# A third raw-weight buffer around the first norm, and a free choice of engine for four low parts

## The chip, the cores and the metric

The kernel runs on one core of one Trainium2 chip. The metric is the device time of one execution in microseconds, as the median of several runs. Inputs, outputs and all arithmetic that counts are 32-bit floating point.

## The reference

A decoder trunk of two layers on 512 tokens of width 1024. Each layer projects x once, runs four groups of attention heads side by side (A forgetting attention, B multi-head latent attention, C stick-breaking attention, D sliding-window attention with grouped keys and values), normalises each group, and sums them through one output projection. A layer norm, a gated feed-forward network of width 2816 and a second layer norm follow.

```python
for l in range(DEPTH):                                  # 2
    h = x @ w_in[l]                                     # split into the inputs of A, B, C, D
    ...                                                 # out_a, out_b, out_c, out_d: (1, 512, 256) each
    y = _group_rmsnorm(concat(out_a, out_b, out_c, out_d), mix_g[l]) @ w_o[l]
    x = _layernorm(ALPHA * x + y, ln1_g[l], ln1_b[l])
    f = (silu(x @ w_gate[l]) * (x @ w_up[l])) @ w_down[l]
    x = _layernorm(ALPHA * x + f, ln2_g[l], ln2_b[l])
```

## The kernel before

**Products in three passes.** TensorE multiplies a 32-bit value as two parts: a high part, which is the value rounded to the faster matmul type (`fp32r`), and a low part, which is the rest. Each product is three passes: high by high, high by low, low by high. So every weight chunk that arrives in a raw buffer is *split*: an engine casts it to the high part (ScalarE mostly, line 722; GpSimd sometimes, line 724), and VectorE or GpSimd subtracts that from the raw value for the low part (line 442). Both parts go into buffers of their own; the raw buffer is free once the low part is done.

**Buffers.** A `Ring` is a set of SBUF buffers. `r_raw` (`w_raw`) has 2 buffers of 128 x 1024 for raw weights, `r_hi` and `r_lo` (`w_hi`, `w_lo`) have 3 each for the parts. `r_qk` has 9 larger ones for queries, keys and later the hidden features. `r_vd` (`vd`) is a single buffer, as large as a raw one: it holds the values of the sliding group D, in both parts; later the paired tiles of the feed-forward network and the second norm's bias vector use it.

**The planner.** The program is written out by a list scheduler that runs when the kernel is built. Each operation has an engine, an estimated cost, the estimated times of what it depends on, and a priority. The scheduler always emits the operation that can start first, engine by engine, and so fixes the order in every engine's queue. On the chip each queue runs in that order, and semaphores hold an operation until its data are there, whatever time was planned for it. The function `best` chooses between engines by the earliest planned end: the later of the time at which the engine has worked off what is queued for it and the time at which the data are there, plus a cost. A low part of 1024 elements costs 69 + 1.042 x 1024 = 1136 ns on VectorE, to which 800 is added in this comparison, and 147 + 2.11 x 1024 = 2308 ns on GpSimd. A split that is further ahead than the next chunk has a low priority (`LOW`): other operations go first.

**Loads and splits.** All weight chunks stand in one list in the order in which TensorE uses them. `loader` loads them in that order, up to five positions ahead of the chunk in use, each when `raw_room` gives a buffer. All loads are issued from SyncE's queue (SP). `splitter` splits them in the same order, up to three positions ahead, each when `room` gives buffers for the parts; the next split starts in the plan only after the low part of the one before has its place.

**The stretch around the first norm.** The dense work of a layer is a list of units in a fixed order, ending its attention part with `wd wc load1 wab`: the output projection of group D, of group C, the load of the norm's vectors, and the projection of groups A and B together. After these come `up(0, 1)`, which computes the first two tiles of 128 hidden features, and then the paired tiles. In `wab` the four chunks of `w_o` belong to A (one of them split into a buffer of `r_v`) and B; it runs over token tiles 0 and 1 (t0, t1) for A then B, and then over t2 and t3. Each result is added onto x by VectorE (line 1743). As soon as a token tile has its four parts, `layernorm` runs on it: sums of squares on ScalarE (line 803), small operations of one element a partition on VectorE, two operations of 128 x 512 to centre and scale (line 853), and two more for the gain and the bias (line 858). TensorE then transposes the tile (line 751, two transposed halves a token tile), and ScalarE and VectorE write the two parts of it to `xT`. `up(0, 1)` uses four chunks, `w_gate` 0, `w_up` 0, `w_gate` 1, `w_up` 1, in that order, for tokens 0 to 255 and then for tokens 256 to 511. Their parts go into buffers of `r_qk`; their splits wait in the plan until group B's normalised output exists (`gate`).

Of the kernel before, what the change touches and what calls it, by code (L numbers as in the profile page):

```python
# [21 lines left out]
F32 = mybir.dt.float32  # L22
# [7 lines left out]
P = 128  # L30
# [16 lines left out]
GA, GB, GC, GD = range(4)  # L47
# [18 lines left out]
E_PE, E_ACT, E_DVE, E_POOL, E_SP = range(5)  # L66
# [11 lines left out]
def join(*deps):  # L78

    if any(x is None for x in deps):  # L80
        return None
    return tuple(map(max, zip(*deps))) if len(deps) > 1 else deps[0]
# [270 lines left out]
def trunk(ctx: ExitStack, tc: tile.TileContext, d):  # L353
# [15 lines left out]
    r_raw = Ring(sb, "w_raw", 2, [P, 1024], F32)  # L369
    r_hi = Ring(sb, "w_hi", 3, [P, 1024], F32R)  # L370
    r_lo = Ring(sb, "w_lo", 3, [P, 1024], F32R)
    r_qk = Ring(sb, "qk", 9, [P, 2, S], F32R)
    r_v = Ring(sb, "v", 2, [P, NT, 4, 2, 64], F32R)
    r_vd = Ring(sb, "vd", 1, [P, NT, 2, 2, 64], F32R)
# [23 lines left out]
    x = const.tile([P, NT, D], F32, name="x_res")  # L398
# [10 lines left out]
    def dma(out, in_, us=0.0, dep=NOW):  # L409

        e = yield Op(E_SP, 450.0, dep)
        nc.sync.dma_start(out=out, in_=in_)
        sched.dma = max(sched.dma, e[E_SP] + 800.0) + us * 1e3
        return mark(E_SP, sched.dma + 1100.0)
# [69 lines left out]
    def rows(src, k0, kt):  # L484
        return src[k0 * P:(k0 + kt) * P].rearrange("(k p) c -> p k c", p=P)
# [6 lines left out]
    class Chunk:  # L492


        def __init__(self, kt, n, parts, custom=None, rings=None, both=None, low=E_POOL, n_split=None, gate=None):
            self.kt, self.n, self.parts, self.custom = kt, n, parts, custom
            self.r_hi, self.r_lo = rings or (r_hi, r_lo)
            self.both, self.n_split, self.low, self.gate = both, n_split or n, low, gate
            self.raw = self.part = self.dep = self.loaded = None

        weight = 1

        def raw_room(self):
            return r_raw.ready()

        def view(self, tile_, n):
            return tile_[:, :self.kt * n].rearrange("p (k n) -> p k n", n=n)

        def load(self):
            self.raw = r_raw.take()  # L510
            e = NOW
            for k0, k1, c0, c1, src in self.parts:
                size = (k1 - k0) * (c1 - c0) * (2 if c1 - c0 < P else 1)
                e = yield from dma(self.view(self.raw.tile, self.n)[:, k0:k1, c0:c1], src, 1.46 * size / 1024, self.raw.dep)
            self.loaded = e
# [171 lines left out]
    def use(chunk):  # L687

        queue["used"] = max(queue["used"], chunk.pos)
        return (yield lambda: chunk.dep)  # L690

    def done(chunk_list, dep):
        for c in chunk_list:
            c.give(dep)

    def dense_op(cost, dep):
        return Op(E_PE, cost, dep, 1)
# [168 lines left out]
    def layer(l):  # L866
# [5 lines left out]
        at = {}  # L872
# [635 lines left out]
        class Uses:  # L1508


            def __init__(self, held, n):
                self.held, self.joint = held, Joint(n, held.give)
# [209 lines left out]
            return out  # L1722


        added = {(t, c): Joint(3) for t in range(NT) for c in range(2)}

        def out_proj(*groups, last=None):

            cs = {g: [Chunk(1, D, [(0, 1, 0, D, rows(d["w_o"][l], 2 * g + k, 1))],
                            both=r_v if len(groups) > 1 and g == groups[0] and k == 0 else None) for k in range(2)]  # L1730
                  for g in groups}
            chunks.extend(c for pair in cs.values() for c in pair)
            blocks = ((0, 1), (2, 3)) if len(groups) > 1 else ((0, 1, 2, 3),)

            def add(g, t, c, ps, dep, st, done_):
                yield lambda: at.get(("rs", g))
                yield lambda: x_dep[t]
                if st is not None:
                    yield lambda: added[t, c].dep
                rs = ops[g][1]  # L1740
                csl = slice(c * 512, c * 512 + 512)
                e = yield Op(E_DVE, 663.0, join(dep, at["rs", g], x_dep[t]))
                DVE.scalar_tensor_tensor(  # L1743
                    out=x[:, t, csl], in0=ps.tile, scalar=rs[:, t:t + 1], in1=x[:, t, csl], op0=ALU.mult, op1=ALU.add,
                    accum_out=st[:, c:c + 1] if st is not None else None,
                )
                ps.give(e)
                if st is not None:
                    done_[c] = e
                    if c == 0:  # L1750
                        last(t, st, e, lambda: done_.get(1))
                else:
                    added[t, c].add(e)

            def unit():
                for half in blocks:
                    for g in groups:
                        final = last if g == groups[-1] else None
                        if half[0] == 0:
                            ready = NOW  # L1760
                            for c in cs[g]:
                                ready = join(ready, (yield from use(c)))
                            yield lambda: at.get(("mix", g))
                        mix = ops[g][0]
                        if final and half[0] == 0:
                            yield lambda: r_b.whole()
                            new_xT(r_b.close())
                        for t in half:
                            st, done_ = None, {}
                            if final:  # L1770
                                yield lambda: NOW if final.loaded else None
                                st = sm.tile([P, 13], F32, name="lnst")
                            for c in range(2):
                                csl = slice(c * 512, c * 512 + 512)
                                yield lambda: r_d.ready()
                                ps = r_d.take()
                                e = yield dense_op(6 * 216.0, join(at["mix", g], ready, ps.dep))
                                for k in range(2):
                                    for i, (a, b) in enumerate(PASSES):
                                        mm(ps.tile, mix.tile[:, k, b, t * P:(t + 1) * P], cs[g][k][a][:, 0, csl],  # L1780
                                           start=(k == 0 and i == 0), stop=(k == 1 and i == 2))
                                spawn(add(g, t, c, ps, e, st, done_), 1 if final is None else 0, 0)
                        if half[-1] == NT - 1:
                            mix.give(e)
                            done(cs[g], e)
            return unit
# [82 lines left out]
        def up(*js):  # L1869
            cs = {}  # L1870
            for j in js:
                for n in ("w_gate", "w_up"):
                    cs[n, j] = Chunk(KT, P, [(0, KT, 0, P, rows(d[n][l][:, j * P:(j + 1) * P], 0, KT))],
                                     rings=(r_qk, r_qk) if len(js) > 1 else None, low=E_DVE if len(js) > 1 else None,
                                     gate=(lambda: ("mix", GB) in at) if len(js) > 1 else None)
            chunks.extend(cs.values())
            toks = HALVES if len(js) > 1 else (ALL,)

            def unit():
                ps, ready = {}, {}  # L1880
                for tok in toks:
                    for j in js:
                        for n in ("w_gate", "w_up"):
                            if tok.start == 0:
                                ready[n, j] = yield from use(cs[n, j])
                                ring = r_d if len(js) > 1 else (r_s if n == "w_gate" else r_u)
                                yield lambda: ring.ready()
                                ps[n, j] = ring.take()
                            xr = yield lambda: x_ready(tok)
                            for k in range(KT):  # L1890
                                e = yield from fm_piece(ps[n, j].tile, cs[n, j], slice(0, P), xs, k, tok, KT, tok.start == 0,
                                                        join(xr, ready[n, j], ps[n, j].dep))
                            if tok.stop == S:
                                done([cs[n, j]], e)
                        if tok.stop < S:
                            continue
                        yield lambda: g_ready(j)
                        gs[j] = g_tile(j)
                        spawn(hidden(j, ps["w_gate", j], ps["w_up", j], e), 0, 0)
            return unit  # L1900
# [230 lines left out]
        low = E_DVE  # L2131
# [140 lines left out]
```

## Time and profile before

| what | value |
|---|---|
| median of 3 runs | 1220.42 us (1219.75 to 1221.94) |
| profiled execution | 1220.06 us, span 1218.3 us |
| mean granted TensorE clock | 0.992 |
| TensorE busy | 1180.2 us, 97% of the span |
| VectorE busy | 892.1 us, 73% |
| ScalarE busy | 685.7 us, 56% |
| GpSimd busy | 241.4 us, 20% |

The span runs from the first to the last instruction of the profiled execution; the time of the execution is a little longer. In the rows below, PE is TensorE's matmuls, PEld its weight loads, DVE VectorE, ACT ScalarE, POOL GpSimd, SP SyncE with the loads that it issues (`SPq`). A row of the timeline gives the start, the time taken, the engine, the line, the operation, what it writes `<-` what it reads, the shape, and in brackets how long the engine had been idle and for what. A row of the waits gives the total in us, how often, and the longest. A row by tile or line gives the count and the least, median and greatest time of one in ns. The first norm of layer 0 lies at about 235 to 270 us, that of layer 1 at about 840 to 875.

### The profile page before, as it was taken

Reading aid. Unit: us, or ns where it says so; the run is one execution under the profiler, and the core shown is the slowest. Engines: PE = TensorE matmul, PEld = TensorE weight load, DVE = VectorE, ACT = ScalarE, POOL = GpSimd, SP = SyncE. Lnnn points to the kernel's source line nnn. Section 1 sums busy time; section 2 is a strip of 40 time slices with the busy share of each in tenths; the row PEclk is TensorE's granted clock in tenths of the full one; section 3 lists DMA queues with packets and bytes.
Section 4 is the critical chain, followed back from the end, with each engine's and each line's share of the span. In section 5 each row is a group of like instructions: output and inputs, shape, how many; then the busy total and the mean of one; then the engine's idle time right before and its main releaser. Section 6 shows DMA issues by size and latency. Waiting matters only on the chain.

```text
span 1218.3 us, 20162 instructions
## 1 busy us (share of the span) xinstructions
PE 1180.2 (97%) x7589; PEld 1069.5 (88%) x7589; DVE 892.1 (73%) x1699; ACT 685.7 (56%) x1441; POOL 241.4 (20%) x243
## 2 busy tenths in 40 slices
PE   8999999989999999999999999999899999999996
PEld 7979878779999989998799797778899989899985
DVE  5669668799896649873655895788998947499626
ACT  4759869456564325553356797684665634256421
POOL 3552765300000000000034536543000000000001
PEclk9999999999999999999999999999999999999999
DMA  6312230423333133324233211203233341343341
GB/s 201 88 47 63 57 104 12 128 87 87 105 105 120 48 128 105 105 92 130 72 71 87 57 53 56 87 27 113 87 90 119 96 131 51 108 119 88 104 138 70
DMA packets 112162, 110.75 MB, mean 91 GB/s; under 512 B 9792, under 2 KB 94656, under 8 KB 112064
## 3 DMA queue, kind: packets, MB, share of 16 engines
q1 hardware_dynamic: 112064, 109.45, 29.9%
q8 instruction: 60, 0.98, 0.3%
q14 instruction: 38, 0.31, 0.1%
HBM read 107.34 MB, written 2.10 MB: 90 GB/s over the span
## 4 chain that ended last, share of the span: by engine, by line
PE 79%; DVE 9%; ACT 5%; issue 3%; POOL 2%; DMA 0%; POOLq 0%; SPq 0%; DVEq 0%; ACTq 0%
PE ps L464 76%; PE ps L1557 1%; DVE x_res L1743 1%; POOL w_lo L442 1%; PE ps L751 1%; DVE xT L442 1%; DVE qk L442 1%; ACT temp L1445 1%; DVE pt L442 1%; ACT pt L1363 1%; DVE x_res L858 1%; ACT xT L722 0%; DVE qk L444 0%; DVE temp L1306 0%; DVE augk L1092 0%
## 5 line engine op out<-in xcount | busy, mean ns | idle before, releaser
L464 PE MATMUL ps<-xT,w_hi 128*128 128x256 f32 (+1 forms) x1128 | 215.5, 318 | 0.0
L464 PEld LDWEIGHTS ps<-xT,w_hi 128*128 128x128 f32 x1128 | 162.4, 191 | 11.4
L464 PE MATMUL ps<-w_hi,qk 128*128 128x512 f32 (+1 forms) x560 | 171.5, 388 | 0.0
L464 PE MATMUL ps<-xT,w_lo 128*128 128x256 f32 (+1 forms) x888 | 166.0, 304 | 0.0
L722 ACT CAST w_hi<-w_raw 128x1024 fp32r<-128x1024 f32 (+2 forms) x91 | 92.8, 1021 | 108.1 <-PE ps L464 90.5
L442 POOL TENSOR_TENSOR w_lo<-w_raw,w_hi 128x1024 fp32r<-128x1024 f32 (+4 forms) x66 | 120.9, 1837 | 106.4 <-ACT w_hi L722 76.3
L442 DVE TENSOR_TENSOR w_lo<-w_raw,w_hi 128x1024 fp32r<-128x1024 f32 x47 | 57.6, 1225 | 111.6 <-ACT w_hi L722 111.5
L464 PEld LDWEIGHTS ps<-xT,w_lo 128*128 128x128 f32 x888 | 123.7, 191 | 7.3
L464 PEld LDWEIGHTS ps<-w_hi,qk 128*128 128x128 f32 x560 | 104.6, 189 | 20.9
L464 PE MATMUL ps<-w_hi,mix 128*128 128x512 f32 x352 | 110.1, 394 | 3.1 <-DVE xT L442 1.8
L464 PE MATMUL ps<-w_lo,qk 128*128 128x512 f32 (+1 forms) x280 | 108.2, 387 | 0.0
L1911 ACT COPY temp<-ps 128x256 f32<-128x256 f32 x120 | 44.7, 373 | 85.2 <-PE ps L464 84.7
L659 ACT CAST w_hi<-temp 128x512 fp32r<-128x512 f32 x78 | 48.3, 620 | 64.9 <-DVE temp L602 35.6
L772 POOL TENSOR_SCALAR x_res<-x_res 128x1024 f32<-128x1024 f32 x8 | 9.4, 1180 | 375.3 <-DVE lnst L840 357.2
L464 PEld LDWEIGHTS ps<-w_hi,mix 128*128 128x128 f32 x352 | 64.6, 188 | 16.4 <-issue 2.1
L442 DVE TENSOR_TENSOR w_hi<-temp,w_hi 128x512 fp32r<-128x512 f32 x78 | 53.2, 687 | 30.7 <-ACT w_hi L659 30.5
L467 POOL TENSOR_TENSOR lnst<-lnst,mhalf 128x1 f32<-128x1 f32 x4 | 3.9, 985 | 362.2 <-DVE lnst L840 362.2
L659 ACT CAST w_lo<-temp 128x512 fp32r<-128x512 f32 x82 | 50.8, 621 | 42.7 <-DVE temp L602 28.1
L464 PE MATMUL ps<-xT,qk 128*128 128x256 f32 x528 | 69.1, 291 | 2.0 <-DVE qk L442 2.0
L464 PE MATMUL ps<-w_lo,mix 128*128 128x512 f32 x176 | 69.0, 392 | 1.9 <-POOL w_lo L442 1.9
L464 PE MATMUL ps<-w_hi,xT 128*128 128x388 f32 (+1 forms) x256 | 69.1, 351 | 0.4 <-DVE qk L444 0.4
L464 PEld LDWEIGHTS ps<-xT,qk 128*128 128x128 f32 x528 | 66.8, 199 | 2.8 <-DVE qk L442 2.6
(234 smaller groups left out, 2692.5 us busy)
## 6 DMA issues: line engine op xcount, KB each, us to landing
w_raw<-in_w_down SPq DMA_DIRECT2D x44, 512.0 KB, 3.8
w_raw<-in_w_in SPq DMA_DIRECT2D x26, 512.0 KB, 3.7
w_raw<-in_w_gate SPq DMA_DIRECT2D x24, 512.0 KB, 3.7
w_raw<-in_w_up SPq DMA_DIRECT2D x24, 512.0 KB, 3.7
w_raw<-in_w_o SPq DMA_DIRECT2D x16, 512.0 KB, 3.7
vd<-in_w_up SPq DMA_DIRECT2D x10, 512.0 KB, 3.7
mixf<-in_w_up SPq DMA_DIRECT2D x10, 512.0 KB, 3.7
vd<-in_w_gate SPq DMA_DIRECT2D x10, 512.0 KB, 4.9
```

Of the source, the lines that this page charges most:

```text
L442: eng.tensor_tensor(out=lo, in0=src, in1=f(hi), op=ALU.subtract)
L464: PE.matmul(out, lhsT=lhsT, rhs=rhs, start=start, stop=stop, skip_group_check=True)
L659: ACT.copy(out=self.part[0], in_=src)
L722: ACT.copy(out=out, in_=in_ if psum is None else psum)
L751: PE.transpose(out=u.tile[:, k * P:(k + 1) * P], in_=x[:, t, kk * P:(kk + 1) * P], identity=ident)
L772: POOL.tensor_scalar(out=x[:, t], in0=x[:, t], scalar1=ALPHA, scalar2=0.0, op0=ALU.mult, op1=ALU.add)
L858: DVE.scalar_tensor_tensor(out=x[:, t, csl], in0=centred[c], scalar=st[:, 9:10], in1=bb[c], op0=ALU.mult, op1=ALU.add)
L1363: ACT.copy(out=dst[0], in_=src)
L1445: ACT.activation(out=p[:, s_], in_=ps.tile[:, s_], func=AF.Exp, bias=r[:, nm + j:nm + j + 1], scale=1.0 if scale is None else scale[:, i:i ...
L1557: PE.transpose(out=u.tile[:, k * P:(k + 1) * P], in_=p.tile[:, k * P:(k + 1) * P], identity=ident)
L1743: DVE.scalar_tensor_tensor(out=x[:, t, csl], in0=ps.tile, scalar=rs[:, t:t + 1], in1=x[:, t, csl], op0=ALU.mult, op1=ALU.add, accum_out=st ...
L1911: ACT.copy(out=dst, in_=src)
```

## The change

Two things change, for eight chunks of each layer: the four `w_o` chunks of `wab` and the four of `up(0, 1)`. First, their raw load may also use the buffer `vd`, once `("mix", GD)` is known to the planner, that is once group D is finished and its values are not needed any more. Second, the low parts of the four chunks of `up(0, 1)`, which were always VectorE's, are given to VectorE or GpSimd by the planner's comparison (`low=None`).

```diff
-        def __init__(self, kt, n, parts, custom=None, rings=None, both=None, low=E_POOL, n_split=None, gate=None):
+        def __init__(self, kt, n, parts, custom=None, rings=None, both=None, low=E_POOL, n_split=None, gate=None, more=None):
...
-            self.both, self.n_split, self.low, self.gate = both, n_split or n, low, gate
+            self.both, self.n_split, self.low, self.gate, self.more = both, n_split or n, low, gate, more
...
+        def raw_rings(self):
+            return (r_raw, r_vd) if self.more and self.more() else (r_raw,)
+
         def raw_room(self):
-            return r_raw.ready()
+            free = [x for r in self.raw_rings() for x in r.free if x is not None]
+            return min(free, key=max) if free else None
...
         def load(self):
-            self.raw = r_raw.take()
+            ring = min((r for r in self.raw_rings() if r.ready() is not None), key=lambda r: max(r.ready()))
+            self.raw = ring.take([P, 1024], F32)
...
+        def vd_free():
+            return ("mix", GD) in at
+
...
             cs = {g: [Chunk(1, D, [(0, 1, 0, D, rows(d["w_o"][l], 2 * g + k, 1))],
-                            both=r_v if len(groups) > 1 and g == groups[0] and k == 0 else None) for k in range(2)]
+                            both=r_v if len(groups) > 1 and g == groups[0] and k == 0 else None,
+                            more=vd_free if len(groups) > 1 else None) for k in range(2)]
...
                     cs[n, j] = Chunk(KT, P, [(0, KT, 0, P, rows(d[n][l][:, j * P:(j + 1) * P], 0, KT))],
-                                     rings=(r_qk, r_qk) if len(js) > 1 else None, low=E_DVE if len(js) > 1 else None,
-                                     gate=(lambda: ("mix", GB) in at) if len(js) > 1 else None)
+                                     rings=(r_qk, r_qk) if len(js) > 1 else None, low=None,
+                                     gate=(lambda: ("mix", GB) in at) if len(js) > 1 else None,
+                                     more=vd_free if len(js) > 1 else None)
```

The work itself, the number of loads and the number of operations stay the same.

## The prediction

> **What bounds the kernel now.** The page's first part was read first, then a table by stretches of time around the first norm of each layer, then the waits of TensorE there.
>
> ```profile
> PE 1180.2 (97%) x7589; PEld 1069.5 (88%) x7589; DVE 892.1 (73%) x1699; ACT 685.7 (56%) x1441; POOL 241.4 (20%) x243
> ```
> TensorE (PE) is busy for 97% of the span of 1218.3 us, so 38 us is all that any edit off TensorE can return. The part of it in reach lies around the first norm. Columns: stretch, its length, then busy time of PE, PEld, DVE (VectorE), ACT (ScalarE), POOL (GpSimd), and the granted TensorE clock.
>
> ```profile
> 204.00:232.00 28.00, 26.80 (x146) 23.01 (x147) 20.64 (x38) 16.81 (x34) 15.45 (x11) 1.00 0.34 105
> 232.00:252.00 20.00, 17.92 (x85) 14.21 (x84) 17.39 (x48) 9.97 (x24) 3.44 (x3) 1.00 0.23 66
> 252.00:268.00 16.00, 12.39 (x95) 11.35 (x94) 14.95 (x34) 8.68 (x20) 0.00 (x0) 1.00 0.27 70
> ```
> From 232 to 268 us VectorE is nearly full and GpSimd nearly empty. The waits of TensorE between 190 and 300 us (total, times, longest), and the one wait of VectorE for another engine between 236 and 268 us:
>
> ```profile
> PE ps L751 <- DVE x_res L858: 2.0, 2, 1.3
> PE ps L464 <- DVE qk L442: 1.6, 2, 1.2
> PE ps L464 <- POOL w_lo L442: 1.4, 1, 1.4
> ```
> ```profile
> DVE x_res L1743 <- PE ps L464: 0.2, 1, 0.2
> ```
> So in this stretch VectorE sets the pace: a microsecond added to its queue before 257 us reaches TensorE whole. In time order, with the wait in brackets:
>
> ```profile
> 257.00 0.63 PE L751 MATMUL ps<-ident,x_res 128*128 128x128 f32 x4 [1.29 <-DVE x_res L858]
> 258.33 0.63 PE L751 MATMUL ps<-ident,x_res 128*128 128x128 f32 x4 [0.70 <-DVE x_res L858]
> 258.72 0.48 PE L464 MATMUL ps<-xT,qk 128*128 128x256 f32 x2
> 259.62 3.13 PE L464 MATMUL ps<-xT,qk 128*128 128x256 f32 x24 [0.43 <-DVE qk L442]
> 263.94 0.74 PE L464 MATMUL ps<-xT,qk 128*128 128x256 f32 x4 [1.19 <-DVE qk L442]
> ```
> These are the transposes of token tile 2 (t2), then the products of w_up 0 and w_gate 1, each late because its low part stands in VectorE's queue. Layer 1 looks alike (its waits between 800 and 910 us give the same first row, 2.0, 2, 1.3), with one difference:
>
> ```profile
> 864.38 5.12 PE L464 MATMUL ps<-xT,qk 128*128 128x256 f32 x28 [0.43 <-DVE qk L442]
> ```
> ```profile
> 864.00:866.00 2.00, 1.61 (x8) 1.62 (x9) 2.00 (x6) 0.76 (x3) 0.00 (x0) 0.62 0.13 34
> 866.00:868.00 2.00, 2.00 (x11) 2.00 (x11) 2.00 (x6) 1.15 (x2) 0.00 (x0) 0.52 0.77 228
> ```
> There the clock fell to 0.52 after the waits for t2, and 28 products took 5.12 us, as long as 3.13, the wait of 1.19 and 0.74 in layer 0.
>
> **The change, part by part.** Loads first. Today's raw loads of the feature tiles, and GpSimd's work in that stretch:
>
> ```profile
> 229.69 0.38 SPq L412 DMA_DIRECT2D w_raw<-in_w_gate  x1
> 234.41 0.38 SPq L412 DMA_DIRECT2D w_raw<-in_w_up  x1
> 236.90 0.37 SPq L412 DMA_DIRECT2D w_raw<-in_w_gate  x1
> 259.63 0.37 SPq L412 DMA_DIRECT2D w_raw<-in_w_up  x1
> ```
> ```profile
> 227.27 2.40 POOL L442 TENSOR_TENSOR w_lo<-w_raw,w_hi 128x1024 fp32r<-128x1024 f32 x1 [0.81 <-ACT w_hi L722]
> 231.02 1.02 POOL L467 TENSOR_TENSOR rsg<-rsg,mhalf 128x4 f32<-128x4 f32 x1 [1.36 <-DVE rsg L1502]
> 232.02 2.37 POOL L442 TENSOR_TENSOR w_lo<-w_raw,w_hi 128x1024 fp32r<-128x1024 f32 x1
> 240.63 1.06 POOL L724 TENSOR_SCALAR qk<-w_raw 128x1024 fp32r<-128x1024 f32 x1 [6.25 <-DMA w_raw<-in_w_gate]
> ```
> ```profile
> L442 DVE TENSOR_TENSOR qk<-w_raw,qk x4: 1207/1211/1219, 235.7 to 265.1; 128x1024 fp32r<-128x1024 f32 x4
> ```
> ```profile
> w_raw<-in_w_gate SPq DMA_DIRECT2D x24, 512.0 KB, 3.7
> ```
> Each load waits for a buffer that a low part gives back: 229.69 follows GpSimd's end at 229.67. The number of loads stays; with `vd` as a third buffer each moves up by about one buffer. SP's queue has nothing else in this stretch but the norm's vectors. The four w_o loads come earlier too. For group B's pair that brings nothing, since their splits wait for w_hi buffers that group C holds until its last product; w_o's second A chunk has its low part earlier, in a stretch where VectorE is busy 20.64 of 28 us. I take 0 for it, and up to 1.0 in the range. `vd` is back long before the second norm and the first paired tiles want it: 0.
>
> w_gate 0 no longer waits for its load. VectorE's adds before the norm, with its idle time in brackets:
>
> ```profile
> 231.92 0.75 DVE L1743 SCALAR_TENSOR_TENSOR x_res<-ps,rsg,x_res 128x512 f32<-128x512 f32 x1 [0.32 <-PE ps L464]
> 234.98 0.75 DVE L1743 SCALAR_TENSOR_TENSOR x_res<-ps,rsg,x_res 128x512 f32<-128x512 f32 x1 [2.31 <-PE ps L464]
> ...
> 237.76 0.75 DVE L1743 SCALAR_TENSOR_TENSOR x_res<-ps,rsg,x_res 128x512 f32<-128x512 f32 x1 [0.15 <-PE ps L464]
> ```
> Its low part (1.21 us) moves from 235.7 into the gaps of 0.32 and 2.31, to about 231.5. The engine is chosen by earliest planned end, 1136+800 ns on VectorE against 2308 on GpSimd, and there GpSimd still has the low part of 232.02 ahead, so VectorE keeps it. It gains VectorE little, since VectorE is waiting for TensorE again at 237.76 (0.15): an estimate of 0.4, a third of the 1.21. Where it starts ahead of GpSimd's 232.02 it can hold that up until 232.7, and TensorE's 1.4 us wait for it with it, by 0.6; or, starting just after it, wait for its end. Which comes first is open; I take the one for layer 0, the other for layer 1.
>
> w_up 0 is decided in the plan just after that, while VectorE still has gaps (2.31): VectorE again, at low priority, and so as late as today. TensorE's 0.43 stays.
>
> w_gate 1 and w_up 1 come after it in the planner, when VectorE's backlog is several operations and GpSimd's queue is empty: GpSimd gets both low parts. Its queue then holds cast, low, cast, low, and runs them as their data land, not at the planned time, as the cast of 240.63 does today on the load of 236.90. With w_gate 1 loaded at about 232.8 to 234.5 and landing 3.7 us later, GpSimd works from about 236.5 or 238.2 on, in the middle of the norm of t0. VectorE loses two low parts, 2.4 us, but late ones; the wait of 1.19 goes in both layers (in layer 1 as part of the 5.12).
>
> Against that stand these rows:
>
> ```profile
> 227.85 2.37 DVE L444 SCALAR_TENSOR_TENSOR mix<-mixf,mg,mix 128x512 fp32r<-128x512 f32 x1
> ```
> ```profile
> 173.71 1.06 POOL L724 TENSOR_SCALAR w_hi<-w_raw 128x1024 fp32r<-128x1024 f32 x1 [2.45 <-PE ps L464]
> ```
> ```profile
> L1313 DVE TENSOR_TENSOR temp<-temp,temp x2: 692/1070/1448, 173.8 to 777.2; 128x512 f32<-128x512 f32 x2
> ```
> ```profile
> 239.06 0.74 DVE L853 SCALAR_TENSOR_TENSOR x_res<-x_res,lnst,lnv 128x512 f32<-128x512 f32 x1
> 239.72 0.21 DVE L840 TENSOR_SCALAR lnst<-lnst 128x1 f32<-128x1 f32 x1
> 239.85 0.74 DVE L853 SCALAR_TENSOR_TENSOR x_res<-x_res,lnst,lnv 128x512 f32<-128x512 f32 x1
> ...
> 241.98 0.74 DVE L858 SCALAR_TENSOR_TENSOR x_res<-x_res,lnst,lnv 128x512 f32<-128x512 f32 x1
> ```
> L444 is the same operation as L853 and L858, on the same size, with two tensors from SBUF. At 227.85 it took 2.37 us, not 0.74, and ended 0.55 after GpSimd's low part. L1313 took 1.45, not 0.69, under a mere cast of GpSimd. So GpSimd's operation, once started, holds up a VectorE operation of this kind until it ends; I take it that it works the other way round too. The worst would be a VectorE waiting through all four GpSimd operations, 2x1.06+2x2.4 = 6.9 us a layer; the replay below has less. The Trainium skill ("SBUF — State Buffer", section "Who interferes with whom") has it that a VectorE instruction with two SBUF inputs and a GpSimd instruction that reads SBUF take turns at a lock, each for its whole length; by that rule too the sum would come out slower.
>
> Replay with w_gate 1 landing at 236.5 (layer 0, TensorE late by the 0.6): cast to 237.6, low to 240.0; the first L853 is held to 240.0 and ends at 240.5. The second cast follows it, 240.5 to 241.5; the second L853 ends at 242.1. The second low runs to 244.4, meanwhile VectorE does what lies between 240.5 and 241.98 today, which reads PSUM or one tensor, then the first L858 is held to 244.4 and ends at 244.9, today 242.7: 2.2 us late. Landing at 238.2 (layer 1, in layer 0's times: GpSimd first, w_gate 0's low part held, its buffer back later): first L853 ends 239.85, low 239.85 to 242.1, second L853 242.7, cast to 243.7, low to 246.0, L858 ends 246.6: 3.9 us late.
>
> What waits for L858 of t0 is a transpose that has no wait today:
>
> ```profile
> 243.00 0.60 PE L751 MATMUL ps<-ident,x_res 128*128 128x128 f32 x4
> ```
> It becomes the new wait, of 1 to 4 us, and everything behind it on VectorE, t2's L858 included, is late by as much. **Sum:** layer 0 +2.2-1.2, layer 1 +3.9-1.2, together +3.7 us. The profiled execution took 1220.06 us (span 1218.3), 0.36 under the median of 1220.42; the forecast against the median is 1224.1. Bounds: per layer between -0.4 (no lock met, w_gate 0's slot gained) and +6.9 (every operation held in full) before the 1.2, so -3.2 to +11.4 in all.
>
> **The rivals.** *Faster.* GpSimd's operations fall where VectorE has no two-tensor operation at hand, or the plan moves the transposes behind other products. Then the 1.19 goes twice, 0.43 twice if w_up 0 goes to GpSimd too, and 0.4 twice at t2 (w_gate 0's slot): -4.0 us, 1216.4. It decides where the lock costs a layer under 1.2 us. For it: L853 and L858 are only 11.8 us of a norm (four tiles, four of 0.74 each), of the 29 from 238 to 267. Against it: they stand at the head of each tile's chain, just where the data land.
>
> *The lows stay on VectorE,* so that only loads move. For it:
>
> ```profile
> L442 DVE TENSOR_TENSOR w_lo<-w_raw,w_hi 128x1024 fp32r<-128x1024 f32 x47 | 57.6, 1225 | 111.6 <-ACT w_hi L722 111.5
> ```
> 44 of these 47 are w_down's, which have the free choice already, and none is on GpSimd. Against it: VectorE has idled 111.5 us before those, and 0.2 here. It gives 1220.4, within 1 us.
>
> *The clock.* If TensorE waits 1 to 4 us at t0 and 2 at t2, the clock may fall as at 866: about 1.3 us more (5.12 against 3.13+0.74) at each of up to two places a layer; at three of the four, 1228.0. By the Trainium skill ("TensorE: Matmul & The Clock Gate", part 1) half rate comes only after an idle window of some 3.4 us; the row of 866 shows it after waits of 1.3 at most, so here the measurement decides. By the rule alone only the wait of 3.9 in layer 1 would cost anything more.
>
> **How the numbers follow.** 0.2% is 2.4 us, about what a measurement of this kernel tells from no change. Forecast (lock outweighs the waits, +2.4 to +6): 0.38. With the clock on top, above +6: 0.10. Nothing to be seen, by lows that stay or by a lock of about 1.2 to 2.4 a layer: 0.31. Faster: 0.21. So faster 0.21, same 0.31, slower 0.48. The range leaves out the far ends of the faster rival and of the clock: 1217.0 to 1228.5; the forecast's own is 1222.8 to 1226.5.
>
> **What would show it.** Two L442 `qk` rows on GpSimd and two on VectorE per layer; L853 or L858 rows of over 1.2 us between 238 and 250; a new wait `PE L751 <- DVE x_res L858` at t0; no 1.19 before w_gate 1; w_up 1 loaded near 235 and not 259.63. The prediction is wrong if GpSimd's operations run with L853 at 0.74, or if the order of TensorE changes before 250 us.

## The result, and the profile after

The changed kernel took 1231.15 us (median of 5 runs, 1229.66 to 1232.58) against 1220.65 for the kernel before: a ratio of 1.0083, with a 95% interval of 1.0072 to 1.0095. The change makes the kernel slower by 10.5 us, where +3.7 was forecast. The profiled execution took 1229.66 us, its span is 1227.9.

ScalarE's table load behind the norm is a landmark that both kernels have. Its rows, the first two of the kernel before, the last two of the changed one:

```profile
275.88 1.28 ACT L1852 ACT_TABLE_LOAD   x1
880.65 1.28 ACT L1852 ACT_TABLE_LOAD   x1
```
```profile
281.51 1.28 ACT L1861 ACT_TABLE_LOAD   x1
889.69 1.28 ACT L1861 ACT_TABLE_LOAD   x1
```
So 5.6 us are lost up to the first norm's end in layer 0, 3.4 more by the same place of layer 1, and 0.6 in all the rest. Not all of this is lost around the norms. The changed kernel is 1.8 us late already where TensorE begins to wait for w_o's last low part in layer 0 (half clock at 76 and 206 us, against once, at 6, in the kernel before), and 4.7 us late at the same product in layer 1. So the profiled execution loses 3.9 us around the norm of layer 0 and 4.3 around that of layer 1, 8.2 together; a good part of the rest of the span's difference is half clock that fell at other places. Lines have moved by 5 to 10: L853, L858, L751 are now L858, L863, L756. The waits of TensorE over the whole span, before and after (total, times, longest):

```profile
PE ps L751 <- DVE x_res L858: 6.1, 5, 2.1
```
```profile
PE ps L756 <- DVE x_res L863: 11.9, 9, 2.2
PE ps L464 <- POOL w_lo L442: 2.5, 2, 2.0
```
The transposes wait 5.8 us longer for the norm's writes, in four more places. In time order, TensorE at w_o's last chunk in the kernel before (first fence), then in the changed one, with the norm of layer 0 and the two transposes of t0 in layer 1:

```profile
234.44 0.50 PE L464 MATMUL ps<-w_lo,mix 128*128 128x512 f32 x1 [1.42 <-POOL w_lo L442]
```
```profile
236.79 0.50 PE L464 MATMUL ps<-w_lo,mix 128*128 128x512 f32 x1 [1.99 <-POOL w_lo L442]
...
248.97 1.44 PE L756 MATMUL ps<-ident,x_res 128*128 128x128 f32 x8 [1.91 <-DVE x_res L863]
255.05 1.38 PE L756 MATMUL ps<-ident,x_res 128*128 128x128 f32 x8 [0.51 <-DVE x_res L863]
...
265.69 6.14 PE L464 MATMUL ps<-xT,qk 128*128 128x256 f32 x39
...
853.85 0.66 PE L756 MATMUL ps<-ident,x_res 128*128 128x128 f32 x4 [1.20 <-DVE x_res L863]
856.60 1.12 PE L756 MATMUL ps<-ident,x_res 128*128 128x128 f32 x4 [2.10 <-DVE x_res L863]
```
t0's transposes had no wait before. What makes them late stands in the rows of GpSimd and VectorE (the first fence is GpSimd's):

```profile
233.80 2.93 POOL L442 TENSOR_TENSOR w_lo<-vd,w_hi 128x1024 fp32r<-128x1024 f32 x1
240.61 1.05 POOL L729 TENSOR_SCALAR qk<-vd 128x1024 fp32r<-128x1024 f32 x1 [3.88 <-DMA vd<-in_w_gate]
241.75 2.39 POOL L442 TENSOR_TENSOR qk<-vd,qk 128x1024 fp32r<-128x1024 f32 x1
244.11 1.50 POOL L729 TENSOR_SCALAR qk<-w_raw 128x1024 fp32r<-128x1024 f32 x1
245.69 2.68 POOL L442 TENSOR_TENSOR qk<-w_raw,qk 128x1024 fp32r<-128x1024 f32 x1
...
848.80 2.80 POOL L442 TENSOR_TENSOR qk<-vd,qk 128x1024 fp32r<-128x1024 f32 x1
```
```profile
233.31 1.21 DVE L442 TENSOR_TENSOR qk<-w_raw,qk 128x1024 fp32r<-128x1024 f32 x1
242.46 2.22 DVE L858 SCALAR_TENSOR_TENSOR x_res<-x_res,lnst,lnv 128x512 f32<-128x512 f32 x1
244.79 1.34 DVE L858 SCALAR_TENSOR_TENSOR x_res<-x_res,lnst,lnv 128x512 f32<-128x512 f32 x1
246.36 0.74 DVE L1752 SCALAR_TENSOR_TENSOR x_res<-ps,rsg,x_res 128x512 f32<-128x512 f32 x1
247.03 1.88 DVE L863 SCALAR_TENSOR_TENSOR x_res<-x_res,lnst,lnv 128x512 f32<-128x512 f32 x1
...
841.88 3.08 DVE L442 TENSOR_TENSOR qk<-w_raw,qk 128x1024 fp32r<-128x1024 f32 x1
849.45 2.71 DVE L858 SCALAR_TENSOR_TENSOR x_res<-x_res,lnst,lnv 128x512 f32<-128x512 f32 x1
853.84 2.71 DVE L863 SCALAR_TENSOR_TENSOR x_res<-x_res,lnst,lnv 128x512 f32<-128x512 f32 x1
```
Operations of 0.74 us take up to 2.71 when a GpSimd operation that reads SBUF is running as they start. L1752, the same operation with one tensor from PSUM, keeps its 0.74 in the middle of a GpSimd low part. GpSimd is held likewise: its low part of 233.80 takes 2.93 beside VectorE's of 233.31, and TensorE waits 1.99 us for it instead of 1.42. In layer 1 GpSimd came first there, and VectorE's low part of 841.88 takes 3.08 instead of 1.21.

The third thing is the clock. Stretches of 2 us of the changed kernel, the granted clock third from the end:

```profile
238.00:240.00 2.00, 2.00 (x6) 1.60 (x5) 0.72 (x4) 0.81 (x2) 0.00 (x0) 0.50 0.92 263
...
856.00:858.00 2.00, 1.40 (x6) 1.30 (x7) 2.00 (x5) 0.24 (x1) 0.00 (x1) 0.50 0.30 49
858.00:860.00 2.00, 2.00 (x6) 1.60 (x5) 2.00 (x7) 0.73 (x3) 0.00 (x0) 0.50 0.63 222
860.00:862.00 2.00, 2.00 (x6) 1.53 (x5) 0.52 (x2) 0.00 (x0) 0.00 (x0) 0.50 0.00 0
```
Right behind the wait of 1.99 and the waits of 1.20 and 2.10 TensorE works at half clock, but not behind the wait of 1.91 (the stretches from 248 to 256 us have 1.00); the 6.14 for 39 products at 265.69 is partly at half clock too. TensorE's busy time times what the clock lacks, summed over the stretches of 2 us below 0.97, is 6.5 us in the kernel before and 9.4 in the changed one.

### The profile page after: what moved, and what is told of

Same layout as the page of the kernel before. It is cut to its first block, busy times and chain, and to the rows that moved or that the text cites. A ratio compares the mean times of both kernels' runs of the same rounds, so it can differ in the third digit from the quotient of the medians.

```text
span 1227.9 us, 20153 instructions
## 1 busy us (share of the span) xinstructions
PE 1184.9 (96%) x7589; PEld 1071.1 (87%) x7589; DVE 899.0 (73%) x1695; ACT 685.8 (56%) x1441; POOL 253.2 (21%) x247
## 4 chain that ended last, share of the span: by engine, by line
PE 78%; DVE 10%; ACT 5%; issue 3%; POOL 2%; DMA 1%; SPq 0%; POOLq 0%; DVEq 0%; ACTq 0%
PE ps L464 76%; PE ps L1562 1%; DVE x_res L1752 1%; DVE x_res L863 1%; DVE qk L442 1%; DVE xT L442 1%; ACT temp L1450 1%; PE ps L756 1%; POOL w_lo L442 1%; ACT pt L1368 1%; DVE pt L442 1%; DMA x_res<-in_x 1%; ACT xT L727 0%; DVE x_res L858 0%; DVE qk L444 0%
## 5 line engine op out<-in xcount | busy, mean ns | idle before, releaser
L442 POOL TENSOR_TENSOR w_lo<-w_raw,w_hi 128x1024 fp32r<-128x1024 f32 (+4 forms) x64 | 116.0, 1820 | 106.7 <-ACT w_hi L727 82.2
```

Source lines behind the costliest of these rows:

```text
L442: eng.tensor_tensor(out=lo, in0=src, in1=f(hi), op=ALU.subtract)
```

## The experiments

Three theories stood. *The lock:* GpSimd's operations beside the norm hold VectorE's, and the transposes come late. *The order:* the earlier loads change TensorE's order (t0's two transposes now stand together), and that costs. *The clock:* half clock, wherever it falls, makes the difference. All runs, with TensorE's wait for the norm's writes and the half clock of the profiled execution, summed as above:

| kernel | median us | ratio to before, 95% interval | wait for the writes, us | half clock, us |
|---|---|---|---|---|
| before | 1220.65 | | 6.1 | 6.5 |
| changed | 1231.15 | 1.0083, 1.0072 to 1.0095 | 11.9 | 9.4 |
| e1_buffer_only | 1223.04 | 1.0018, 1.0006 to 1.0030 | 6.1 | 6.5 |
| e2_choice_only | 1225.59 | 1.0032, 1.0018 to 1.0045 | 9.4 | 4.9 |
| e3_write_only | 1221.64 | 0.9999, 0.9988 to 1.0011 | 6.5 | 6.7 |
| e4_twice | 1237.24 | 1.0120, 1.0096 to 1.0145 | 13.3 | 14.2 |
| e5_write_both | 1219.00 | 0.9990, 0.9979 to 1.0001 | 6.2 | 8.1 |
| e6_fill_before | 1219.40 | 0.9991, 0.9981 to 1.0000 | 1.3 | 3.4 |
| e7_fill_after | 1226.82 | 1.0042, 1.0029 to 1.0055 | 3.1 | 5.1 |
| e8_timed | 1225.32 | 1.0029, 1.0019 to 1.0040 | 6.9 | 9.8 |
| e9_timed_before | 1221.77 | 1.0004, 0.9994 to 1.0014 | 6.1 | 8.4 |
| e10_timed_fill | 1219.87 | 0.9987, 0.9976 to 0.9998 | 1.3 | 5.1 |
| e11_write_long | 1222.01 | 1.0010, 0.9996 to 1.0023 | 6.5 | 3.2 |
| e12_one_operand | 1226.33 | 1.0038, 1.0025 to 1.0051 | 9.0 | 8.0 |

The medians are of 5 to 12 runs. Each ratio is to the kernel before as it was measured beside that kernel, with medians of 1220.65 to 1221.39; the last two columns are of one execution each, and half clock differs from one execution to the next.

**The two halves of the change.** The third buffer with all low parts on VectorE (e1), and the free choice without the buffer (e2):

```diff
-   rings=(r_qk, r_qk) if len(js) > 1 else None, low=None,
+   rings=(r_qk, r_qk) if len(js) > 1 else None, low=E_DVE if len(js) > 1 else None,   # e1, in the changed kernel
```
```diff
-   rings=(r_qk, r_qk) if len(js) > 1 else None, low=E_DVE if len(js) > 1 else None,
+   rings=(r_qk, r_qk) if len(js) > 1 else None, low=None,                              # e2, in the kernel before
```


> The third raw buffer and the gate for it stay as in the changed kernel; all four low parts of the first feature tiles go back to VectorE as in the kernel before. If GpSimd's low parts beside the norm make the loss (the lock theory), it is gone here but for GpSimd's two casts: 1218 to 1222 us, VectorE's norm writes (L863) of 0.6 to 0.8 us, no wait over 1 us of a first transpose for them. If the earlier loads and the order that they give TensorE make the loss (the order theory: both transposes of token tile 0 together, the clock dropping behind them), it stays: 1228 to 1232. If drops of the clock alone make it (the clock theory), the time is anywhere in 1219 to 1230 and goes with the number of drops in the trace.

> The kernel before with nothing but the free choice between GpSimd and VectorE for the first feature tiles' low parts; loads stay late, in two buffers. Only w_gate 1's low part goes to GpSimd. Lock theory: one GpSimd low part of 2.4 us a layer beside the norm's scales or writes costs about half of what two cost, 1222 to 1226. Order theory: the loads have not moved, so no loss, 1219 to 1222. Clock theory: by the number of drops, 1219 to 1226.

e1 lost 2.2 us, e2 4.8. In e1 VectorE's writes are at 0.74, and t0's transposes stand together without a wait, so the price of the order is at most about those 2.2 (0.7 to 3.7 by the interval). In e2 nothing but w_gate 1's low part has changed engine. GpSimd's row, then VectorE's, then TensorE's:

```profile
241.44 2.37 POOL L442 TENSOR_TENSOR qk<-w_raw,qk 128x1024 fp32r<-128x1024 f32 x1
```
```profile
241.54 2.81 DVE L858 SCALAR_TENSOR_TENSOR x_res<-x_res,lnst,lnv 128x512 f32<-128x512 f32 x1
```
```profile
244.41 0.66 PE L751 MATMUL ps<-ident,x_res 128*128 128x128 f32 x4 [1.69 <-DVE x_res L858]
```
A write that starts 0.1 us after GpSimd's low part takes 2.81 us, and the transpose behind it, which waited for nothing, waits 1.69; 1.58 in layer 1. That alone is a slower kernel, with none of the four loads earlier and with less half clock than before.

**The lock by itself.** The order of all instructions stays that of the changed kernel; GpSimd's two low parts of a layer become writes of zeros (e3), or are computed twice (e4). e11 makes the writes as long as the low parts, e12 puts two casts there.

```diff
-   split_lo(engines[low], lo[:, cs], raw[:, cs], hi[:, cs])
+   # for GpSimd's low parts of the gated chunks alone:
+   POOL.memset(f(lo[:, cs]), 0.0)                             # e3: once; e11: three times
+   split_lo(POOL, ...); split_lo(POOL, ...)                   # e4
+   POOL.tensor_scalar(out=lo[:, cs], in0=raw[:, cs], ...)     # e12: twice
```


> The changed kernel, instruction for instruction in the same order, but GpSimd's two low parts of a layer (w_gate 1, w_up 1) are replaced by writes of zeros, which read nothing; those low parts are left out of the result. Lock theory: VectorE's scales and writes of the norm no longer wait for GpSimd; the up unit starts 2 to 4 us earlier in each layer, 1223 to 1227. Order theory: TensorE's order is the same, so 1229 to 1232. Clock theory: the waits of the transposes for the norm's writes shrink below what lets the clock drop, so a drop a layer (1.5 to 2.9 us) may go with them, 1224 to 1231.

> The changed kernel in the same order, with each of GpSimd's two low parts of a layer (w_gate 1, w_up 1) computed twice in a row, 2.4 to 2.9 us more of GpSimd each. Lock theory: VectorE's norm operations lose up to the doubled stretch again, and the second write of the pair is late for the first transposes of token tiles 0 and 1: 2 to 5 us more a layer, 1235 to 1241. Order theory and clock theory: nothing but GpSimd is longer and the low parts are wanted only at the up unit, so 1229 to 1234.

> e3 left open whether its writes of zeros won because they read nothing or because they are short (0.96 us against 2.4 to 2.9). Here each of GpSimd's two low parts of a layer is three writes of zeros in a row, 2.9 us, as long as the held low parts of the changed kernel; those low parts are left out of the result. Lock theory: VectorE is held by what GpSimd reads or works through two operands, not by its being busy: 1220 to 1223, VectorE's scales and writes at 0.74 us while GpSimd writes. Rival, length (the second cast, the raw tiles' release and the loads behind them come later): 1228 to 1231.

> As e11, but each low part is two casts in a row (one operand read, one written, 1.05 us each), 2.1 us together; those low parts are copies of the raw weights in the result. If any GpSimd operation that reads SBUF holds VectorE's two-operand operations, as the 1.1 to 1.4 us of scales beside a single cast suggest: scales and writes of 1.5 to 2.2 us, 1226 to 1230. If it takes two operands on both sides: 1220 to 1223.

e3 gives back 9.5 us, more than the lock theory's own 4 to 8, and e4 loses 6.1 more, with 4.8 us more of half clock. In e11 GpSimd is busy as long as in the changed kernel and the time is e3's (9.1 given back), so what counts is that GpSimd reads SBUF, not that it is busy. Its rows (GpSimd, then VectorE):

```profile
238.74 2.99 POOL L553 MEMSET qk<- 128x1024 f32 x3
241.70 1.05 POOL L733 TENSOR_SCALAR qk<-w_raw 128x1024 fp32r<-128x1024 f32 x1
```
```profile
240.50 0.75 DVE L862 SCALAR_TENSOR_TENSOR x_res<-x_res,lnst,lnv 128x512 f32<-128x512 f32 x1
242.15 1.14 DVE L867 SCALAR_TENSOR_TENSOR x_res<-x_res,lnst,lnv 128x512 f32<-128x512 f32 x1
```
The scale at 240.50, within the writes, takes 0.75; the write at 242.15, within the cast, takes 1.14. And e12, with nothing but casts, keeps 4.9 us of the loss: an operation with one operand holds VectorE too, only more briefly. The order theory falls with these runs: TensorE's order is the changed kernel's in all of them, and the intervals of e3 and e11 include the time of the kernel before.

**The other meeting.** e3 was still 2.6 us above its like in which VectorE's low part of w_gate 0 is a write of zeros as well:

```diff
+   if self.gate is not None and low == E_DVE and self.first:
+       DVE.memset(f(lo[:, cs]), 0.0)                          # first: w_gate 0
```


> As e3 (GpSimd's two low parts are writes of zeros), and VectorE's low part of w_gate 0, which ran beside GpSimd's low part of the last w_o chunk, is a write of zeros too; all three are left out of the result, the order of the instructions is the same. Theory GB: that meeting is what is left of the loss in layer 0: GpSimd's low part takes 2.4 instead of 2.9 us, TensorE's wait for it 1.4 instead of 2.0, and the half clock right behind it (1.6 us in e1, e3, e4 and the changed kernel, none in the kernel before and e2, where that wait is 1.42) does not come: 1219 to 1220.5. Rival: drops of the clock come by themselves, not by that wait: 1221 to 1222, as e3.

e5 took 1219.0 against e3's 1221.6. GpSimd's low part of the last w_o chunk takes 2.37 again, and:

```profile
234.94 0.50 PE L464 MATMUL ps<-w_lo,mix 128*128 128x512 f32 x1 [1.44 <-POOL w_lo L442]
```
The wait for this product is 1.99 to 2.00 us in seven of the fourteen kernels (changed, e1, e3, e4, e7, e11, e12), and half clock follows within 5 us in all seven. It is 1.42 to 1.44 in the other seven, and in none of them does half clock follow. So by the rows this meeting costs 0.57 us of wait and some 1.6 of half clock, 2.2 together. The times agree but do not settle the size: the medians of e3 and e5 differ by 2.6 us, the ratios by 0.0009, which is 1.1 us, and their intervals overlap. e5's runs reach from 1216.42 to 1222.44.

That half clock follows the longer wait holds for this place; it is no rule by length. Before and after, at the sums of squares 30 us earlier (the first fence is the kernel before):

```profile
205.20 1.05 PE L464 MATMUL ps<-ones,temp 128*128 128x1 f32 x8 [1.29 <-POOL temp L732]
206.11 2.74 PE L464 MATMUL ps<-pt,v 128*128 128x512 f32 x16
```
```profile
205.42 1.05 PE L464 MATMUL ps<-ones,temp 128*128 128x1 f32 x8 [1.28 <-POOL temp L737]
206.34 4.30 PE L464 MATMUL ps<-pt,v 128*128 128x512 f32 x16
```
The same wait of 1.28 is followed by half clock in the changed kernel (4.30 us for the same 16 products) and not in the kernel before; it is in six of the fourteen traces.

**The clock.** Transposes of the identity fill TensorE's waits, in a plan that stays as it was.

```diff
     e = yield Op(E_PE, 4 * 107.0, join(u.dep, dep))
+    for k in range(idle):
+        PE.transpose(out=u.tile[:, k % 4 * P:(k % 4 + 1) * P], in_=ident, identity=ident)
```


> The kernel before, plan unchanged, with transposes of the identity (0.1 us each, overwritten by what follows) that fill TensorE's waits at four places: token tile 2 of the first norm in both layers (9 and 4 into waits of 1.29 and 0.70), token tile 2 of the second norm of layer 0 (16 into 2.15), the sum of squares in layer 1 (16 into 2.19). Clock theory: TensorE is busy there, the clock does not drop at 608, 756 and 866 us, 1.6 us each: 1215 to 1217.5. If such waits don't set the clock, or these transposes don't count as work for it: 1220 to 1222, and the drops stay.

> The changed kernel, plan unchanged, with the same filling transposes, and more of them in token tile 0's waits of the first norm (14 in layer 0; 9 and 14 in layer 1), where VectorE's writes are late. The lock stays (VectorE's writes of 1.9 to 2.7 us). Clock theory: the drops at 264 to 270 and 854 to 864 us go (1.4 and 4.1 us in its trace) and those at 613 and 760 of other executions: 1223 to 1227. If the loss is the lock's waits alone: 1230 to 1232.

At the filled places the clock stayed at 1.00 in e6, e7 and e10. e7 gave back 4.3 us, so about two fifths of the loss went with the half clock; 1.3 of that is what e6's filling brings the kernel before. e6 itself is a miss: of three drops of some 1.6 us only 1.3 us came back. Its stretch in layer 1, and what stands there now (in the kernel before this product, at half clock, had no wait):

```profile
866.00:868.00 2.00, 2.00 (x19) 2.00 (x18) 2.00 (x6) 0.86 (x3) 0.00 (x0) 1.00 0.80 227
```
```profile
869.48 0.74 PE L464 MATMUL ps<-xT,qk 128*128 128x256 f32 x4 [1.19 <-DVE qk L442]
```
TensorE at full clock arrives early and waits for VectorE's low part of w_gate 1: the half clock there had been nearly free. That accounts for one of the three drops; where the rest of the other two went is not shown.

**Keeping the engines apart.** e8 is the changed kernel with two one-column reads that are meant to put the low parts where the other engine has no two-tensor work, and with w_up 1's on VectorE. e9 is the kernel before with w_gate 1's low part alone moved in this way; e10 adds e6's filling.

```diff
+   if self.after is not None:          # a one-column read ahead of the low part
+       low, when, src = self.after
+       a = yield Op(low, 130.0, join(dep, a, (yield when)), prio)
+       engines[low].tensor_scalar(out=seen, in0=src(), scalar1=1.0, scalar2=0.0, ...)
    ...
+   cs["w_gate", js[0]].after = E_DVE, (lambda: gb.dep), (lambda: f(gb.part[1][:, D - 1:D]))              # e8
+   cs["w_gate", js[1]].after = E_POOL, (lambda: at.get(("written", 1))), (lambda: x[:, 1, D - 1:D])      # e8, e9, e10
+   cs["w_up", js[0]].low = cs["w_up", js[1]].low = E_DVE                                                  # e8
```


> The changed kernel with all low parts computed, but kept apart from two-operand work on the other engine: VectorE's low part of w_gate 0 waits for GpSimd's low part of the last w_o chunk (a one-column read of it ahead), GpSimd's low part of w_gate 1 waits for the norm's last write of token tile 1 (a one-column read of x), and w_up 1's low part is VectorE's, as before. If the two meetings make the whole loss: 1218 to 1220.5, with neither the 2.0 wait for w_lo nor a 1.2 wait for w_gate 1. If the earlier loads cost something of themselves (1223 in e1 without any low part on GpSimd): 1222 to 1224.

> The kernel before with one thing moved: w_gate 1's low part goes to GpSimd, but only after the norm's last write of token tile 1 (a one-column read of x ahead of it), so at 248.5 to 250.9 us, where VectorE runs no operation with two operands in SBUF until the scale at 252.2. Lock theory: nothing is held, VectorE's scales and writes stay at 0.74 us, and the wait of 1.19 us for w_gate 1 in layer 0 goes (in layer 1 half clock hides it): 1218.5 to 1220. Rival: some other thing is late there next (w_up 0's low part, w_up 1's load): 1220.5 to 1222.

> e9 with e6's filling transposes. In e6 the half clock at 866 us was gone and a wait of 1.19 us for w_gate 1 stood in its place in layer 1; here that wait is gone in both layers: 1216 to 1218, below the kernel before. Rival: what the filling brings is given back to the next wait again: 1218.5 to 1220.

In e9 the lock theory holds in every row (GpSimd's low part at 250.90 takes 2.39, all scales and writes 0.74 or 0.75), the wait of 1.19 is gone, and the time is the same. The next thing is late: the first weights of the paired feature tiles, with no wait before.

```profile
288.32 2.90 PE L465 MATMUL ps<-v,w_hi 128*128 128x256 f32 x22 [0.95 <-DVE w_hi L443]
```
In e8, which missed its forecast by 5 us, that wait stands too, in both layers, and the cast of w_up 1, freed by the later low part, now meets the scales of t2 (GpSimd, VectorE, TensorE):

```profile
253.81 1.06 POOL L736 TENSOR_SCALAR qk<-w_raw 128x1024 fp32r<-128x1024 f32 x1
```
```profile
254.27 1.14 DVE L865 SCALAR_TENSOR_TENSOR x_res<-x_res,lnst,lnv 128x512 f32<-128x512 f32 x1
```
```profile
259.50 0.63 PE L763 MATMUL ps<-ident,x_res 128*128 128x128 f32 x4 [1.69 <-DVE x_res L870]
```
1.69 instead of e5's 1.30. Against e5's span (1223.8 to 1219.0), twice 0.4, twice 0.95 and 1.7 more half clock make 4.4 of the 4.8 us. e10 is the only version below the kernel before with an interval that excludes 1, by 0.13%, less than the 0.2% that a measurement here can tell; no version clearly beats the kernel before.

## Why the prediction was right or wrong, point by point

**Loads.** Right in kind: each moved up a buffer, w_up 1 was issued at 237.23 instead of 259.63. w_gate 1 was issued at 236.76, 2 to 4 us later than the replay had it. In layer 0 the norm was late as well, and GpSimd's work fell on the operations of the replay: both scales and the first write of t0 (2.22, 1.34 and 1.88 us). In layer 1 it fell on the second scale and the second write (2.71 each).

**w_gate 0.** Right: VectorE kept the low part, moved it into the gap (233.31), and it held GpSimd's low part of the last w_o chunk in layer 0 by 0.57 us (0.6 forecast), not in layer 1, where VectorE was held instead (3.08 us). What was missed is the half clock behind the wait of 1.99: 2.2 us by the rows, where the replay counted 0.6.

**w_up 0, w_gate 1, w_up 1.** Right: two low parts on each engine. The 0.43 stayed only in layer 1.

**The lock.** Right in kind and nearly in size. t0 and t1 wait 1.91+0.51 in layer 0 (2.2 forecast) and 1.20+2.10 in layer 1 (3.9). The rule of the Trainium skill ("SBUF — State Buffer", section "Who interferes with whom") agrees with the runs down to a detail that e11 tested: by that section a GpSimd instruction that only writes SBUF doesn't contend, and beside e11's writes VectorE's scale took 0.75.

**The wait of 1.19.** It went in both layers, but the 2.4 us set against the lock were more than a removed wait is shown to bring: in layer 1 the kernel before had half clock in its place. e9 removes it and gains nothing, since the pair's weights are late next; e5, which also has the earlier loads and none of the meetings, gained 1.7, with an interval that just reaches no change. The step named no next wait.

**The order of TensorE** changed before 250 us, which the prediction had named as something that would make it wrong. By e3, e5 and e11 it cost nothing that these runs can tell.

**The step that failed is the sum: it left the clock out, as a rival with a chance of 0.10.** The mechanism of the lock was the right one. The forecast put waits of 2.2 and 3.9 us where there were none, and its own row of 866 showed half clock after waits of 1.29 and 0.70; the half clock behind the new waits was then a term of the sum, not a case beside it. The rows of the two profiled executions show the size. In layer 0 waits of 0.57 (1.99 instead of 1.42), 1.91 and 0.51 us come in, and waits of 0.66, 0.43 and 1.19 go: +0.7, where +1.0 was forecast. Half clock adds 1.6 behind the wait of 1.99 and 1.5 at 264, behind t2's two waits; 0.7+3.1 is 3.8 of the 3.9 lost there. In layer 1 waits of 1.20 and 2.10 come in and one of 0.66 goes: +2.6, where +2.7 was forecast. Half clock adds 2.9 behind the new waits, and the 1.6 behind t2's waits is gone; 2.6+1.3 is 3.9 of the 4.3 lost there. t2's waits are as long as before, and their half clock has only changed the layer. So what the forecast's +3.7 lacks is the 4.5 us of half clock behind the new waits, and with them it is the 8.2 that the two norms lost. These are one execution of each kernel; what the medians differ by beyond 8.2 isn't put down to a row.

By the runs, from the changed kernel downward: 9.5 us are the two low parts on GpSimd (e3), 5.4 of them waits for the writes (11.9 to 6.5 us), some 3.0 half clock (e7's 4.3 less e6's 1.3), and 1.1 not put down to a row; 2.6 are the meeting at w_o's last chunk (e5), with the doubt said there; what is left is 1.7 faster than before. These are differences of one median from the next, so that they add up to the 10.5 us is no test of them. The rival's price, 1.3 at three places, was short in the same way: 1.6 a drop, and 2.9 in layer 1, where two waits followed each other and the clock stayed at 0.50 from 856 to 862 us (the 4.1 in e7's expectation was too high).

By the rule of the Trainium skill ("TensorE: Matmul & The Clock Gate", part 1), half rate comes after an idle window of some 3.4 us. Half clock stood behind every wait of 1.99 to 2.00 for w_o's last low part, so the measurement decides against that length; where half clock falls is still open, as the last section says.

## What to carry to other kernels

Before work is moved to GpSimd, list what VectorE runs with two tensors from SBUF at that time: each such meeting costs the rest of GpSimd's operation, cast or subtraction, and here 2.4 us a layer taken off VectorE brought 5.4 us of waits in the two layers. A new wait of TensorE near 2 us is to be priced with the half clock that may stand behind it, some 1.6 us, as a term of the sum: in the fourteen traces 26 of 37 waits of 1.88 us or more have half clock begin at their end or within 3 us of it. And where a wait is removed, look for the next late thing: e9 took 1.19 us away and found 0.95 of it 25 us further on.

## What the runs showed of the hardware that was not expected

At w_o's last low part a wait of TensorE of 1.99 to 2.00 us was followed by half clock in seven kernels of seven, and one of 1.42 to 1.44 in none of seven. No length parts the two elsewhere: waits of 1.20 to 1.30 at 75 and 205 us, each with 1.05 us of products of a single column behind it, were followed by half clock in seven and in six of the fourteen traces, and the new wait of 1.91 at t0 in the changed kernel was not. Two waits away from the change, of 2.15 us (at 608) and 2.19 (at 754), dropped the clock in the kernel before; in the changed kernel they are 2.15 and 2.18, and it did not drop. The Trainium skill ("TensorE: Matmul & The Clock Gate", part 1) has the window free-running, so that where a wait falls in it differs from run to run. That would fit; no run here shows the window itself.

A held VectorE operation is recorded from its start, the hold included, and it starts 0.2 us before GpSimd's record ends: 849.45+2.71-0.74 = 851.42 against 848.80+2.80 = 851.60 in the changed kernel, 241.54+2.81-0.74 = 243.61 against 241.44+2.37 = 243.81 in e2. So, for an operation that would have begun within GpSimd's row, the time at which it gets through can be worked out from that row alone.
